# Where the token sums of products by seven are made, and which tiles become such products, in a one-layer Hyena and attention kernel

## The chip, the core and the metric

The kernel runs on one core of one Trainium2 chip. The core has five engines that each take their own instructions in order and wait for one another by semaphores: TensorE (PE, matrix products into PSUM), VectorE (DVE, elementwise work), ScalarE (ACT, copies, tanh, exp), GpSimd (POOL) and SyncE (SP, which issues most DMAs). The metric is the device time of one execution in microseconds. Before the change it is 885.33 us, the median of three runs (885.21 to 885.59).

## The reference, cut to what matters

One layer of a network with two parallel branches, for 128 context tokens and 512 latent tokens (640 columns in all, `NT`), model width 1024:

```python
h = x * (1 + scale) + shift
(v_h, x1, x0, g_h), (q, k, v, g_a), m = split_projection(h, w_in, conv_w, conv_b)
y_h = hyena_long_conv(v_h, x1, x0, h_fwd, h_bwd, hyena_d)
y_a = neighbourhood_attention(q, k, v, ctx_k, ctx_v, rpb)   # the context tokens: context_attention
p_h = (y_h * silu(g_h)) @ w_bh
p_a = (y_a * silu(g_a)) @ w_ba
out = (sigmoid(m)[h] * p_h + sigmoid(m)[a] * p_a) @ w_out
x_new = layer_norm(ALPHA * x + gate * out)
```

`w_in` has 80 tiles of 128 output columns: 32 for the Hyena branch, then 8 each for queries, keys, values, attention gates and the two mixing gates. Everything is float32.

## The kernel before, in words

**Precision.** Each float32 operand of a product is split into a high part (`fp32r`, which the matrix engine multiplies in one pass) and a low part, the rest. A product is three passes: high by high, high by low, low by high. A plain tile of 128 output columns for 640 tokens is 8 blocks of the inner dimension x 3 passes x 2 halves of 320 tokens = 48 matmuls (`accumulate`, L168; with the low passes last, L182). The weight's split costs an ACT copy (high) and a DVE subtraction (low) on 128x1024 (`split`, L100 to L102). With `eng="dma"` (`wtile`, L145 to L149) ACT writes the negated weight into the low tile, ACT writes the high tile, and a DMA issued by POOL adds the weight from memory into the low tile, so that DVE does nothing. Raw tiles have two buffers, high tiles two, low tiles three.

**Products by seven.** `pair_tile` (L1110) makes two weight tiles together by a Strassen-like scheme on 2 x 2 blocks (two halves of the inner dimension, two weight tiles, two halves of the tokens): 7 products of 12 matmuls, 84 in place of 96. It needs sums of token blocks (`token_sums`, L1026, t1 to t4, each with a high and a low part, in two rounds r = 0 and 1 of two blocks each) and sums of weight blocks (`prepare` and `wsum`, L1078 to L1108, all four on DVE). The seven products come in the order b11, t2, t3, t1, b21, t4, b22 (`ORDER`, L1069); b's are the tokens themselves. The weight sums of a pair named in `runs` (L1186) are made in advance, when the pair ahead of it has done its fourth product; a first pair of a run makes its own when it starts. Before the change the 8 mixing pairs, query and key 3 to 7 (one pair each) and the gate pairs from 2 to 7 are made so: 16 pairs.

**Order of the work.** After a prologue (modulation, hidden layers of the filters, first tiles), four quarters of the Hyena branch run: projections, short convolution, and a long convolution by small Fourier matrices (`long_conv`, `long_conv_back`). The last quarter's long convolution is woven (`weave`, L68: so many steps of the side work per step of the main work) into `hand_over` (L841): the last projections, then query 0, key 0, values 0, gate 0, query 1 as plain tiles, then values 1 and key 1 with round 0 of the token sums beside them. `attention_setup` (L854), which comes last in the side chain, gives the convolution's memory back (`hy.close()`) and opens the pools `sp`, `tp` and `at` there; the scratch rows of the token sums (L1034) lie in `sp`, the bias tiles in `at`. Then the attention stage (L1254) goes through eight pairs of heads; the main work of each, `mains(j)` (L1242), is woven with scores, softmax and values. In the first of them, gate 1, query 2 and key 2 are plain tiles with round 1 of the token sums beside them. After attention come the two branch projections, the output projection and the norm.

In the attention stage PE's order is as the program writes it (`manual_schedule`); elsewhere, and on the other engines except for pinned instructions, a scheduler chooses the order when the program is built, by its own model of durations, and the engines then keep to it. So the instruction order of both programs on each engine is known without running them.

Of the kernel before, what the change touches and what calls it, by code (L numbers as in the profile page):

```python
# [18 lines left out]
NK = 8  # L19
# [26 lines left out]
def tile_hyena_natten_step(ctx: ExitStack, tc: tile.TileContext, a, o):  # L46
# [668 lines left out]
    def chain(*gens):  # L715
        for g in gens:
            yield from g
# [47 lines left out]
            nc.vector.scalar_tensor_tensor(ql[:, cs], src[:, ss], scale(cs), f(q[:, cs]), op0=ALU.mult, op1=ALU.subtract)  # L765

    def queries(j):
        for hf, p in enumerate((yield from proj(T_Q + j, low_last=True))):
            q_half(j, hf, p[:, :HALF])
        yield  # L770

# [27 lines left out]

    def keys(j):  # L800
        cached_keys(j)
        for hf, p in enumerate((yield from proj(T_K + j, low_last=True))):
            k_half(j, hf, p[:, :HALF])
        yield

    def values(m):
        w = [wtile(T_V + 2 * m + i, width=256) for i in range(2)]
        ps = [acc(f"v{m}_{i}") for i in range(2)]
        v = slot(m, "v", f"v{m}")
        out[f"v{m}"] = v  # L810

        def passes(k):
            wh, wl = w[k // 4][0][k % 4], w[k // 4][1][k % 4]
            return ((hH, wh, k == 0, False), (hL, wh, False, False), (hH, wl, False, k == NK - 1))

        for half in range(2):
            ks = range(4 * half, 4 * half + 4)
            for k in ks:
                for x, wk, first, last in passes(k):
                    for t in range(4):  # L820
                        nc.tensor.matmul(  # L821
                            ps[t // 2][:, t % 2 * 256 : t % 2 * 256 + 256], x[:, k, P * t : P * t + P], wk,
                            start=first and t % 2 == 0, stop=last, skip_group_check=True,
                        )
                yield
            if half:
                for i in range(2):
                    nc.scalar.activation(v[:, 512 * i : 512 * i + 512], ps[i][:], AF.Copy)
            else:
                pe = acc(f"ve{m}")  # L830
            for k in ks:
                for x, wk, first, last in passes(k):
                    nc.tensor.matmul(pe[:, :256], x[:, k, P * 4 :], wk, start=first, stop=last, skip_group_check=True)  # L833
            yield
        nc.scalar.activation(v[:, 1024:], pe[:, :256], AF.Copy)
        nc.sync.dma_start(o["new_v"][:, m * 256 : m * 256 + 256], v[:, :256])
        yield
# [3 lines left out]
    def hand_over():  # L841
        yield from quarter_tail(3)
        hwa_stack.close()
        out["slots_l"] = left.enter_context(tc.tile_pool(name="slots_l", bufs=1))
        out["slots_q"] = left.enter_context(tc.tile_pool(name="slots_q", bufs=1))
        yield from chain(queries(0), keys(0), values(0), gate_a(0), queries(1))
        out["slots_r"] = left.enter_context(tc.tile_pool(name="slots_r", bufs=1))
        yield from alongside(chain(values(1), keys(1)), token_sums(0), 2)

    tail = ctx.enter_context(ExitStack())  # L850
    ac = ctx.enter_context(ExitStack())
# [2 lines left out]
    def attention_setup():  # L854
        nonlocal at, sp, tp
        hy.close()
        sp = ac.enter_context(tc.tile_pool(name="sp", bufs=1, side="right"))
        tp = left.enter_context(tc.tile_pool(name="tp", bufs=1))
        at = ac.enter_context(tc.tile_pool(name="at", bufs=1, side="right"))
        biases[0] = [bias_tile(h) for h in range(2)]  # L860
        for b, c in ((0, 0), (3, 320)):
            for h in range(2):
                edges[b, h] = at.tile([P, 384], F32, tag=f"edge{b}{h}", name=f"edge{b}{h}")
                nc.gpsimd.memset(edges[b, h][:, c : c + 64], 0.0)
        yield

    at = sp = tp = None

# [145 lines left out]

    N_ATT = 4

    def gate_a(j):
        out[f"sg{j}"] = sg = at.tile([P, NT], F32, tag="sg", bufs=2, name=f"sg{j}") if j else row(yhp, "yh", "sg0")
        yield from gate_tile(T_GA + j, sg[:], low_last=True)
        yield  # L1020


    SUMS = ("t1", "t3", "t2", "t4")
    tok = {t: [[], []] for t in SUMS}

# [52 lines left out]
    def prepare(i0, i1, pin):  # L1078
# [8 lines left out]

        def wsum(j, x, y, op, dst=None):
            src[j] = dst if dst is not None else row(sp, "s", f"s{j}_{i0}", bufs=2)[:, :512]
            ins = nc.vector.tensor_tensor(src[j], x, y, op=op)  # L1090
            if pin and j == 2:
                tc.keep_in_program_order(ins)

# [88 lines left out]
    def mix_(m):  # L1182
# [1 line left out]
        return t, t + 1  # L1184

    runs = (  # L1186
        (mix_(0), qk_(3), mix_(1), qk_(4), ga_(2)), (mix_(2), qk_(5), mix_(3), ga_(4), qk_(6)),
        (mix_(4), qk_(7), mix_(5), ga_(6), mix_(6), mix_(7)),
    )
    follow = {x: y for run in runs for x, y in zip(run, run[1:])}  # L1190
# [6 lines left out]
        for _ in side:  # L1197
            pass

    weave(hand_over(), chain(long_conv(3), long_conv_back(3), attention_setup()), 6 * NK + N_VALUES, N_CONV + N_BACK + 1)  # L1200

    def yh_home(i):
        if i < 4:
# [37 lines left out]

    def mains(j):  # L1242
        return {
            0: ((alongside(chain(gate_a(1), queries(2), keys(2)), token_sums(1), 2, 5),), 3 * NK),
            1: ((mix(0), queries_keys(3)), 2 * N_PAIR),
            2: ((mix(1), queries_keys(4), gates_a(2)), 3 * N_PAIR),
            3: ((values(2), mix(2)), N_VALUES + N_PAIR),
            4: ((queries_keys(5), mix(3), gates_a(4)), 3 * N_PAIR),
            5: ((queries_keys(6), values(3), mix(4)), N_VALUES + 2 * N_PAIR),
            6: ((queries_keys(7), mix(5), gates_a(6)), 3 * N_PAIR),  # L1250
# [313 lines left out]
```

## Time and profile before

| what | value |
|---|---|
| timed runs | 885.21, 885.33, 885.59 us |
| profiled execution, span from first to last instruction | 883.0 us |
| its own time | not listed apart; 2.3 us lie between its span and the median above |
| PE busy | 871.0 us, 6522 matmuls |
| DVE / ACT / POOL busy | 632.7 / 429.5 / 128.8 us |
| mean granted clock of PE | 0.998 |
| end of the Hyena projections on PE | 308.4 us |
| first attention scores on PE | 386.2 us |
| first matmuls of a product by seven | 411.1 us |

The table takes its first rows from the times and the page, the last three from the chain of waits and the clock from the list of cores. PE's busy time counts a matmul from start to end, and matmuls overlap; what one costs is the distance from one start to the next.

### The profile page before, as it was taken

To read this page: it belongs to the slowest core of one execution; us is meant where nothing else is said; L and a number is where in the kernel's file an instruction comes from. 1 tells how busy PE (TensorE), PEld (TensorE's weight loads), DVE (VectorE), ACT (ScalarE), POOL (GpSimd) and SP (SyncE) were. 2 spreads that over 40 slices of the span, in tenths; PEclk is the share of its full clock that TensorE was granted. 3 is DMA by queue.
4 is the path that set the end of the run, shared out by engine and by line. 5 is a ranking of instruction groups with operands and counts; after the bars stand their busy time and mean duration, and the time that the engine had idled before them with its cause. 6 is when DMAs were issued, how large, how long until landed. Compare 5 with 4: busy or idle time off the path is not lost.

```text
span 883.0 us, 16773 instructions
## 1 busy us (share of the span) xinstructions
PE 871.0 (99%) x6522; PEld 843.5 (96%) x6522; DVE 632.7 (72%) x1247; ACT 429.5 (49%) x919; POOL 128.8 (15%) x130
## 2 busy tenths in 40 slices
PE   8999999999999999999999999999999999999996
PEld 7899999999999999999999999999999999999885
DVE  5576693795668478699787567865788567676656
ACT  4486454655545432356665465555666632243200
POOL 1111010010101000024423222222222200000000
PEclk9999999999999999999999999999999999999999
DMA  9976666565656231253525153433252478545511
GB/s 325 401 164 148 134 136 126 132 140 118 168 112 142 70 108 55 72 195 105 164 80 169 55 152 100 142 105 122 80 181 83 132 285 283 181 152 198 214 64 55
DMA packets 54986, 129.07 MB, mean 146 GB/s; under 512 B 8283, under 2 KB 24283, under 8 KB 54908
## 3 DMA queue, kind: packets, MB, share of 16 engines
q1 hardware_dynamic: 45260, 107.62, 37.1%
q0 software_dynamic: 4032, 14.68, 10.2%
q10 hardware_dynamic: 5616, 5.70, 1.9%
q8 instruction: 51, 0.84, 0.4%
q14 instruction: 27, 0.22, 0.1%
HBM read 113.83 MB, written 14.16 MB: 145 GB/s over the span
## 4 chain that ended last, share of the span: by engine, by line
PE 96%; DMA 3%; DVE 1%; SPq 0%; issue 0%; DVEq 0%
PE mm L168 37%; PE sp L1125 23%; PE mm L182 6%; PE out L1391 6%; PE v L821 5%; PE pt L918 3%; PE s L925 2%; PE s L878 2%; DMA ada<-wada 2%; PE ve L833 1%; DMA xt<-xT 1%; PE yb L158 1%; PE yb L156 1%; PE fl L453 1%; PE yb L157 1%; PE ut L601 1%
## 5 line engine op out<-in xcount | busy, mean ns | idle before, releaser
L1125 PE MATMUL sp<-t,wb 128*128 128x320 f32 x768 | 120.6, 310 | 0.0
L1125 PEld LDWEIGHTS sp<-t,wb 128*128 128x128 f32 x768 | 113.8, 188 | 0.5 <-issue 0.5
L168 PE MATMUL mm<-hL,wh 128*128 128x320 f32 x480 | 113.8, 312 | 0.0
L168 PE MATMUL mm<-hH,wh 128*128 128x320 f32 x480 | 113.3, 312 | 0.3 <-ACT hH L365 0.3
L168 PE MATMUL mm<-hH,wl 128*128 128x320 f32 x480 | 111.4, 310 | 0.0
L1125 PE MATMUL sp<-hH,wb 128*128 128x320 f32 x384 | 93.2, 313 | 0.0
L168 PEld LDWEIGHTS mm<-hH,wh 128*128 128x128 f32 x480 | 80.5, 188 | 2.2 <-issue 1.2
L168 PEld LDWEIGHTS mm<-hL,wh 128*128 128x128 f32 x480 | 81.0, 188 | 1.2 <-DVE hL L373 0.4
L168 PEld LDWEIGHTS mm<-hH,wl 128*128 128x128 f32 x480 | 80.6, 188 | 0.3
L1125 PEld LDWEIGHTS sp<-hH,wb 128*128 128x128 f32 x384 | 66.1, 188 | 1.9 <-issue 1.9
L900 POOL TENSOR_SCALAR p<-p,sm 128x384 f32<-128x384 f32 x32 | 46.5, 1462 | 111.8 <-DVE sm L899 98.1
L101 ACT ACTIVATE wh<-raw 128x1024 fp32r<-128x1024 f32 x31 | 32.8, 1059 | 59.2 <-PE mm L168 23.8
L1125 PE MATMUL sp<-hL,wb 128*128 128x320 f32 x192 | 59.3, 309 | 0.0
L148 POOL DMA_DIRECT2D wl<-wall x28 | 24.3, 869 | 226.6 <-ACT wl L147 159.3
L102 DVE TENSOR_TENSOR wb<-s,wb 128x512 fp32r<-128x512 f32 x64 | 44.0, 701 | 15.8 <-ACT wb L101 15.7
L101 ACT ACTIVATE wb<-s 128x512 fp32r<-128x512 f32 x64 | 39.1, 629 | 27.7 <-DVE s L1090 21.5
L101 ACT ACTIVATE wb<-raw 128x512 fp32r<-128x512 f32 x48 | 30.1, 628 | 34.1 <-PE sp L1125 22.0
L102 DVE TENSOR_TENSOR wl<-raw,wh 128x1024 fp32r<-128x1024 f32 x31 | 37.9, 1221 | 12.0 <-ACT wh L101 11.9
L149 ACT ACTIVATE wh<-raw 128x1024 fp32r<-128x1024 f32 x28 | 29.7, 1060 | 33.1 <-PE mm L168 33.0
L1391 PE MATMUL out<-woh,yhs 128*128 128x512 f32 (+1 forms) x176 | 45.5, 372 | 0.0
L900 POOL TENSOR_SCALAR edge<-edge,sm 128x320 f32<-128x320 f32 x32 | 42.5, 1339 | 1.9 <-DVE sm L899 1.9
L168 PE MATMUL mm<-yhs,wh 128*128 128x320 f32 x224 | 41.9, 309 | 0.0
(364 smaller groups left out, 2160.5 us busy)
## 6 DMA issues: line engine op xcount, KB each, us to landing
raw<-wall SPq DMA_DIRECT2D x93, 512.0 KB, 3.6
wl<-wall POOLq DMA_DIRECT2D x28, 512.0 KB, 5.7
ada<-wada SPq DMA_DIRECT2D x16, 512.0 KB, 6.7
tm<-bias SPq DMA_DIRECT2D x16, 512.0 KB, 4.9
gate<-wgate SPq DMA_DIRECT2D x8, 512.0 KB, 4.0
wo<-wall SPq DMA_DIRECT2D x8, 512.0 KB, 4.5
xt<-xT SPq DMA_DIRECT2D x8, 320.0 KB, 7.0
dec<-decay SPq DMA_DIRECT2D x20, 128.0 KB, 5.1
```

Of the source, the lines that this page charges most:

```text
L101: hi = nc.scalar.activation(dst_h, src, AF.Copy)
L102: return hi, (eng or nc.vector).tensor_tensor(dst_l, src, f(dst_h), op=ALU.subtract)
L148: nc.gpsimd.dma_start(wl, a["wall"][i], accum_op=ALU.add)
L149: nc.scalar.activation(wh, raw[:], AF.Copy)
L168: nc.tensor.matmul(ps[hf][:, :HALF], wt[k], x[:, hf * HALF : (hf + 1) * HALF], start=(i == 0 and k == 0), stop=(i == lead[2] and k == NK - ...
L182: nc.tensor.matmul(p[:, :HALF], w[i // 2][k], (hH, hL)[i % 2][:, k, cs], start=n == 0, stop=n == len(steps) - 1, skip_group_check=True,)
L821: nc.tensor.matmul(ps[t // 2][:, t % 2 * 256 : t % 2 * 256 + 256], x[:, k, P * t : P * t + P], wk, start=first and t % 2 == 0, stop=last, ...
L878: nc.tensor.matmul(dst[h], x[rows(h), qs], y[rows(h), ks], start=i == 0, stop=i == 2, skip_group_check=True)
L900: nc.gpsimd.tensor_scalar_mul(pv, pv, sm[:, 2:3])
L918: nc.tensor.transpose(pt[:, i * P : i * P + P], x, ident)
L1125: nc.tensor.matmul(dst, wk, x(xi, k), start=j < 4 and k == 0 and i == 0, stop=k == 3 and i == 2, skip_group_check=True,)
L1391: ins = nc.tensor.matmul(dst, m[k][:, c0 : c0 + P], w[:, c : c + n], start=(first and k == 0), stop=(last and k == 5), skip_group_check=True,)
```

## The change

- Query 0, key 0 and all values get their low halves by accumulating DMA (`eng="dma"`).
- `hand_over` ends with values 0. `attention_setup` is no longer a step of the woven side chain but is called after it. Then comes a new `first_head`: query 0, key 0 and values 1, with both rounds of the token sums beside them, one step of the sums for each step of the tiles.
- Gates 0 and 1, query and key 1, and query and key 2 become products by seven; `gate_a` for single gate tiles goes. The main work of the first heads is rearranged.
- Of the four weight sums of a pair, sums 3 and 6 are made on POOL.

```diff
     def queries(j):
-        for hf, p in enumerate((yield from proj(T_Q + j, low_last=True))):
+        for hf, p in enumerate((yield from proj(T_Q + j, eng="dma", low_last=True))):
...
     def keys(j):
...
-        for hf, p in enumerate((yield from proj(T_K + j, low_last=True))):
+        for hf, p in enumerate((yield from proj(T_K + j, eng="dma", low_last=True))):
...
     def values(m):
-        w = [wtile(T_V + 2 * m + i, width=256) for i in range(2)]
+        w = [wtile(T_V + 2 * m + i, "dma", width=256) for i in range(2)]
...
-        yield from chain(queries(0), keys(0), values(0), gate_a(0), queries(1))
+        yield from values(0)
+
+    def first_head():
         out["slots_r"] = left.enter_context(tc.tile_pool(name="slots_r", bufs=1))
-        yield from alongside(chain(values(1), keys(1)), token_sums(0), 2)
+        yield from alongside(chain(queries(0), keys(0), values(1)), chain(token_sums(0), token_sums(1)), 1)
...
-            ins = nc.vector.tensor_tensor(src[j], x, y, op=op)
+            ins = (nc.gpsimd if j in (3, 6) else nc.vector).tensor_tensor(src[j], x, y, op=op)
...
     runs = (
-        (mix_(0), qk_(3), mix_(1), qk_(4), ga_(2)), (mix_(2), qk_(5), mix_(3), ga_(4), qk_(6)),
+        (ga_(0), qk_(1), qk_(2), mix_(0), mix_(1), qk_(3), ga_(2)), (mix_(2), qk_(4), qk_(5), mix_(3), ga_(4), qk_(6)),
...
-    weave(hand_over(), chain(long_conv(3), long_conv_back(3), attention_setup()), 6 * NK + N_VALUES, N_CONV + N_BACK + 1)
+    weave(hand_over(), chain(long_conv(3), long_conv_back(3)), 4 * NK + N_VALUES, N_CONV + N_BACK)
+    attention_setup()
+    for _ in first_head():
+        pass
...
-            0: ((alongside(chain(gate_a(1), queries(2), keys(2)), token_sums(1), 2, 5),), 3 * NK),
-            1: ((mix(0), queries_keys(3)), 2 * N_PAIR),
-            2: ((mix(1), queries_keys(4), gates_a(2)), 3 * N_PAIR),
-            3: ((values(2), mix(2)), N_VALUES + N_PAIR),
+            0: ((gates_a(0), queries_keys(1)), 2 * N_PAIR),
+            1: ((queries_keys(2), mix(0)), 2 * N_PAIR),
+            2: ((mix(1), queries_keys(3), gates_a(2)), 3 * N_PAIR),
+            3: ((values(2), mix(2), queries_keys(4)), N_VALUES + 2 * N_PAIR),
```

In the changed program `prepare` and its sums are at L1073 to L1103 (`wsum` at L1085), `pair_tile`'s matmuls at L1120, `token_sums` at L1021 to L1056.

More of the change, by code (lines that the diff above doesn't have):

```diff
@@ L864, in attention_setup @@
                 nc.gpsimd.memset(edges[b, h][:, c : c + 64], 0.0)
-        yield
     at = sp = tp = None
@@ L1015, in tile_hyena_natten_step @@
     N_ATT = 4
[L1017 to L1020, printed above, removed]
     SUMS = ("t1", "t3", "t2", "t4")
```

## The prediction

> **What bounds the kernel now.** I read the page first, then the waits of TensorE (PE), then the chain of work that ended last, and only then the other engines, in the one stretch that the change rebuilds.
>
> ```profile
> span 883.0 us, 16773 instructions
> PE 871.0 (99%) x6522; PEld 843.5 (96%) x6522; DVE 632.7 (72%) x1247; ACT 429.5 (49%) x919; POOL 128.8 (15%) x130
> ```
>
> ```profile
> PE adaT L249 <- DMA ada<-wada: 1.8, 3, 0.9
> PE adaT L266 <- POOL spare L308: 1.5, 1, 1.5
> ```
>
> The second fence is the top of PE's waits (line waited for: us in total, times, longest). The largest entries belong to the prologue and are under 2 us; none comes from the middle of the kernel. The chain of waits says the same and gives PE's pace (start us, us, what):
>
> ```profile
> 308.40 1.32 PE mm L182 x9
> ...
> 373.80 0.87 PE y L696 x8
> ...
> 376.83 1.44 PE ve L833 x12
> ...
> 386.19 1.50 PE s L878 x16
> ...
> 439.48 6.17 PE sp L1125 x42
> ...
> 705.18 91.51 PE mm L168 x624
> ```
>
> So the chain runs on PE without holes. A matmul of 320 columns costs 91.51/624 = 0.147 us (6.17/42 agrees), one of 256 columns 1.44/12 = 0.12, a transpose 0.87/8 = 0.11. The "mean ns" of the page, about 310, is latency and is no price. Any matmul less is time won, and any moment in which PE's next operand is not ready is time lost.
>
> **What is removed.** Three pairs of plain tiles (gates 0 and 1, query and key 1, query and key 2) become products by seven: 3 x 96 matmuls go, 3 x 84 come. That is 36 x 0.147 = **-5.3 us** if PE stays fed. With a span of 883.0, 2.3 us under the median of 885.33, this alone would give 880.0.
>
> **What is moved.** A pair's second product reads t2 of both rounds of token sums (`k // 2` picks the round), so now the first pair, gates 0 and 1, needs all sums of both rounds, and its own weight sums behind them. In before, plain tiles (gate 1, query 2, key 2) covered round 1, and half of round 0 lay beside key 1. The sums' scratch lies in pool `sp`, which opens only when the long convolution has given its memory back. The order in which the changed program issues DVE's work settles where they stand (position, line, output<-input; abridged):
>
> ```
> 400 L102 pl_4 (last half of the last long convolution)
> 401-410 L689, L698, L524, L528 (u and yh, ten instructions)
> 411 L1038 ts<-hH,hL (first token sum)
> ...
> 450 L102 t_11 (t2, round 1, low half)
> 453 L102 t_11 (t4, round 1, low half)
> 454 L1085 s_56 (weight sum 1)
> 455 L102 wb_1 (its low half)
> ```
>
> The same listing gives PE: values 1, the first half of product 0, the back transform's last 18 matmuls, 10 transposes, 18 score matmuls, the second half of product 0, then product 1, which waits for ACT's copy of position 454. DVE takes its instructions in this order, so all 26 sums lie on the path.
>
> *When product 0 is half done.* In before PE went from 308.40 to 386.19, 77.8 us, without a hole. The changed order has, up to that half product, 150 fewer plain matmuls (246 down to 96; 22.0 us), 18 matmuls of 256 columns and 10 transposes not yet done (2.2 and 1.1), and 6 new ones (0.9): 77.8 - 22.0 - 2.2 - 1.1 + 0.9 = 53.4, so 361.8.
>
> *When the long convolution ends.* The groups of DVE between 371 and 412 us and the split's price on both engines (busy us, mean ns):
>
> ```profile
> L102 DVE TENSOR_TENSOR t<-ts,t 128x640 fp32r<-128x640 f32 x8 | 6.7, 834 | 0.8 <-ACT t L101 0.8
> L1032 DVE TENSOR_TENSOR ts<-ts,hH 128x640 f32<-128x640 f32 x4 | 3.4, 859 | 0.0
> L1032 DVE TENSOR_TENSOR ts<-ts,hL 128x640 f32<-128x640 f32 x4 | 3.3, 816 | 0.0
> L698 DVE SCALAR_TENSOR_TENSOR u<-u,hyd,y 128x512 f32<-128x512 f32 x2 | 2.2, 1148 | 0.0
> L893 DVE CUSTOM_DVE_ANT_0 p<-s,tm 128x384 f32<-128x384 f32 x4 | 2.0, 544 | 0.0
> L1045 DVE TENSOR_TENSOR ts<-ts,hH 128x640 f32<-128x640 f32 x2 | 1.9, 931 | 0.1
> L893 DVE CUSTOM_DVE_ANT_0 edge<-s,tm 128x320 f32<-128x320 f32 x4 | 1.8, 478 | 0.0
> L1043 DVE TENSOR_TENSOR ts<-hH,hL 128x640 f32<-128x640 f32 x2 | 1.7, 870 | 0.0
> L1046 DVE TENSOR_TENSOR ts<-ts,hL 128x640 f32<-128x640 f32 x2 | 1.6, 820 | 0.0
> L1050 DVE TENSOR_TENSOR ts<-hH,ts 128x640 f32<-128x640 f32 x2 | 1.6, 818 | 0.0
> L1051 DVE TENSOR_TENSOR ts<-ts,hL 128x640 f32<-128x640 f32 x2 | 1.6, 812 | 0.0
> ...
> L528 DVE TENSOR_TENSOR yh<-yh,u 128x64 f32<-128x64 f32 (+1 forms) x4 | 1.4, 415 | 0.0
> L798 DVE TENSOR_TENSOR kl<-ck,k 128x128 fp32r<-128x128 f32 x4 | 1.3, 356 | 0.0
> ...
> L899 DVE RECIPROCAL sm<-sm 128x1 f32<-128x1 f32 x8 | 0.9, 145 | 0.2 <-ACT p L898 0.2
> L1090 DVE TENSOR_TENSOR s<-s,raw 128x512 f32<-128x512 f32 x1 | 0.7, 693 | 0.0
> ...
> L689 DVE SCALAR_TENSOR_TENSOR u<-u,hyd,yp 128x128 f32<-128x128 f32 x2 | 0.6, 344 | 0.0
> L524 DVE TENSOR_TENSOR yh<-yh,u 128x128 f32<-128x128 f32 x2 | 0.5, 280 | 0.0
> L945 DVE TENSOR_REDUCE smp<-s 128x1 f32<-128x128 f32 x2 | 0.5, 281 | 0.0
> ```
>
> ```profile
> L101 ACT ACTIVATE wb<-s 128x512 fp32r<-128x512 f32 x64 | 39.1, 629 | 27.7 <-DVE s L1090 21.5
> ```
>
> The first transform group's last matmul stands 15 matmuls (2.0 us) before 361.8, at 359.8. Only then are its operand buffers free: copies and subtractions of the next two (0.63 + 2 x 0.65) to 361.7, 12 matmuls to 363.2, beside them copy and subtraction of the last operand (0.63 + 0.69) to 363.8, 6 matmuls to 364.5, a copy (0.4, an estimate from the 0.63 for twice the columns) and 2 + 8 transposes to 366.0. DVE's ten instructions (0.6 + 2.2 + 0.5 + 1.4) start at 365.2 and end at **370.0**.
>
> *From there to position 454.* The 26 sums and low halves are 6.7 + 3.4 + 3.3 + 1.9 + 1.7 + 3 x 1.6 = 21.8 us. Among them stand four of the eight score minima (2.0/2 + 1.8/2 = 1.9), two reductions (0.5), reciprocals (0.5), two L798 (0.7) and two weight sums (1.4). Together 26.8, less about 1.8 because consecutive rows overlap slightly in time: **25.0**. One load adds to it: the bias tiles stand behind the yh stores in SP's queue, which go out at 370.0, and by the row below land 4.9 us later, 375.0, where DVE arrives at about 374.2; I take 1.0. Position 454 then ends at 396.0, ACT's copy at **396.7**, and only then does product 1 start. PE's own work between 361.8 and there is 2.2 + 1.1 + 1.5 (scores) + 0.9 = 5.7 of 34.9 us: **29.2 us** of hole.
>
> ```profile
> tm<-bias SPq DMA_DIRECT2D x16, 512.0 KB, 4.9
> wl<-wall POOLq DMA_DIRECT2D x28, 512.0 KB, 5.7
> ```
>
> **After the hole.** A hole this long has a second price. PE's clock and its first work (windows: times, PE, PEld, DVE, ACT, POOL busy, clock; timeline of the prologue):
>
> ```profile
> 880.00:883.00 3.00, 0.00 (x0) 0.00 (x0) 0.00 (x0) 0.00 (x0) 0.00 (x0) 0.50 0.41 139
> ```
>
> ```profile
> 1.54 3.66 PE L266 MATMUL adaT<-hid 128*128 128x256 f32 x16 [1.54 <-POOL spare L308]
> ```
>
> A few us after the last matmul the granted clock is 0.50, and the first 16 matmuls of the kernel take 3.66/16 = 0.23 us instead of 0.12. So about 3.6 us at half pace follow the hole: 1.8 us lost. The Trainium skill (TensorE: Matmul & The Clock Gate, "What's actually happening") puts both the fall and the recovery at about one window of 3.4 us, which would make an estimate of 1.7 us; the trace agrees, though before has no hole in its middle to show it there.
>
> The third product needs a weight sum that POOL now makes, after another one that waits for product 1's low half:
>
> ```profile
> 31.23 1.38 POOL L300 TENSOR_TENSOR wl<-raw,wh 128x512 fp32r<-128x512 f32 x1 [8.42 <-ACT wh L296]
> ```
>
> ```profile
> 394.59 4.73 POOL L900 TENSOR_SCALAR p<-p,sm 128x384 f32<-128x384 f32 x2
> ...
> 421.88 2.46 POOL L900 TENSOR_SCALAR p<-p,sm 128x384 f32<-128x384 f32 x2
> ```
>
> A POOL operation on 512 columns took 1.38 against 0.69 on DVE, and POOL's rows stretch from 1.23 to 2.37 each where DVE is full of sums. Two of them (2.8 to 4.8), a copy and a subtraction end 5 to 7 us after 396.0, while PE at half pace arrives about 6 us after it: 0.4 us (0 to 3). The Trainium skill (SBUF — State Buffer, "Who interferes with whom") says that a DVE operation with two SBUF inputs and a GpSimd operation that reads SBUF block each other for a whole instruction; the 4.73 against 2.46 fits. In later pairs both sums are begun about six products (6 x 12 x 0.147 = 10.6 us) ahead of their use, so I cost them at nothing; without that cover each pair would pay up to 2 us.
>
> The ten new accumulating DMAs land 5.7 us after issue. In the new order values 0 and 1, query 0 and key 0 have their raw tile a whole tile (7 us or more) ahead; if one is late by 2 us, PE loses it before a point where it waits for DVE anyway. The DVE work that goes (16 low halves, 32 weight sums) lies where PE was never waiting for it, so its gain is nothing.
>
> **The sum.** -5.3 + 29.2 + 1.8 + 0.4 = +26.1. Against the profiled span: 883.0 + 26.1 = 909.1, and with the 2.3 us around it **911.4; I predict 911**. Bounds: DVE may reach the first sum at 368 or 372, its stretch may take 24 or 28 (POOL normalises probabilities beside it), the restart 0 to 5, values 2 and 3 with their DMAs in POOL's queue 0 to 2. Together that is 905 to 920.
>
> **Rivals.**
> ```profile
> 342.86 2.83 DVE L641 TENSOR_TENSOR X<-X,F 128x2560 f32<-128x2560 f32 x1
> ```
>
> 1. *The sums do lie beside the tiles* (the side on which it is not slower). If DVE came to its first sum about 26 us before PE has finished product 0 at 367.5 (361.8 + 5.7), that is before some 342 us, the hole would vanish and 880 remain. For it speaks that the change lists the sums beside query 0, key 0 and values 1; against it the issue order and the memory that the last convolution holds: in before the convolution is still at its spectrum's product at 342.86 (the row above). Break-even is a hole of 5.3 us. Chance 0.04, and 0.01 for a draw.
> 2. *The hole is half filled*: DVE runs the convolution's end much earlier than PE's order suggests, and the hole is 10 to 20 us: 891 to 903. Against it: the relay above is set by PE's own order. 0.06.
> 3. *POOL sums late in every pair*: 19 pairs at 1 to 2 us on top of my sum, 930 to 949. For it: 4.73 us for two operations; against it 10.6 us of lead. By the cited rule of blocking, each of two operations would wait for one DVE operation of 0.7 more, 1.4 us, still inside the lead. 0.05.
> 4. My forecast, 903 to 925: 0.84.
>
> The range 903 to 920 holds a little over 8 in 10 of this. A measurement of this kernel can tell about 0.2% (1.8 us) from no change. Faster 0.04, same 0.01, slower 0.95.
>
> **What would show it.** Right: PE's waits, empty in the middle until now, hold one entry of 20 us or more at product 1 of the first pair, with ACT's wb or DVE as its releaser; the first token sum starts near 370 and the last weight sum before it ends near 396; the clock's row there falls to 0.50 and recovers; from the second pair on PE runs at 0.147 again. Wrong: token sums before 350 us, a hole under 15 us, or PE waits on POOL repeated through the attention stage.

## The result, and the profile after

The changed kernel takes **927.81 us** (median of 4 runs, 926.71 to 928.03), the kernel before 885.27 (4 runs, 884.69 to 885.59): a ratio of 1.0482, 95% interval 1.0469 to 1.0495, or 42.5 us more. The profiled execution has a span of 926.3 us against 883.0, 43.3 us more. The forecast was 911 us with a range of 903 to 920: the side was right, the size was not.

The page of the changed kernel, whose rows answer to the page of before:

```profile
span 926.3 us, 16823 instructions
...
PE 875.2 (94%) x6486; PEld 844.8 (91%) x6486; DVE 637.4 (69%) x1241; ACT 448.2 (48%) x945; POOL 186.2 (20%) x178
...
PE   8999999999999999068999999999999999999996
...
PEclk9999999999999999578999999999999999999999
```

PE has 36 matmuls fewer, as counted, and is 94% busy instead of 99%. The 17th and 18th of the 40 slices (each 23.2 us) show the hole, and in the 17th the granted clock is down to half. PE's waits (line, waited for, us in total, times, longest), of which before had nothing beyond the prologue:

```profile
PE sp L1120 <- ACT wb L101: 28.8, 1, 28.8
PE s L879 <- DVE kl L793: 3.7, 2, 1.9
PE pt L919 <- DVE sm L894: 2.1, 1, 2.1
...
PE v L821 <- DMA wl<-wall: 1.8, 1, 1.8
...
PE s L879 <- DVE u L698: 0.8, 1, 0.8
PE pt L919 <- ACT pts L921: 0.7, 1, 0.7
PE yp L686 <- ACT yep L682: 0.5, 1, 0.5
PE yb L157 <- DVE pl L102: 0.3, 1, 0.3
```

These nine waits are 38.8 us (the unrounded entries of the timeline): 28.8 at product 1 of the first pair (its second product; the first is product 0), 1.6 shortly ahead of it (the rows that end in u, yep and pl), and 8.4 behind it. The account of the span is then: -5.3 us for 36 matmuls, +38.8 us of waits, and by subtraction 43.3 + 5.3 - 38.8 = 9.8 us in which PE works, but more slowly than before. Of the waits the prediction has only the first, and in its bounds that of the values.

VectorE's stretch in the timeline of the changed kernel (start, duration, line, output<-input, in brackets idle time before it and what ended that):

```profile
370.11 0.84 DVE L1038 TENSOR_TENSOR ts<-hH,hL 128x640 f32<-128x640 f32 x1
...
374.89 0.49 DVE L894 CUSTOM_DVE_ANT_0 edge<-s,tm 128x320 f32<-128x320 f32 x1 [0.82 <-DMA tm<-bias]
...
382.16 1.09 DVE L1027 TENSOR_TENSOR ts<-ts,hH 128x640 f32<-128x640 f32 x1
383.28 1.19 DVE L1027 TENSOR_TENSOR ts<-ts,hL 128x640 f32<-128x640 f32 x1
385.27 0.83 DVE L102 TENSOR_TENSOR t<-ts,t 128x640 fp32r<-128x640 f32 x1 [0.80 <-ACT t L101]
...
397.36 0.82 DVE L102 TENSOR_TENSOR t<-ts,t 128x640 fp32r<-128x640 f32 x1 [0.80 <-ACT t L101]
398.21 0.69 DVE L1085 TENSOR_TENSOR s<-s,raw 128x512 f32<-128x512 f32 x1
```

And PE behind it:

```profile
399.62 7.90 PE L1120 MATMUL sp<-t,wb 128*128 128x320 f32 x36 [28.81 <-ACT wb L101]
```

The first token sum stands at 370.1 and weight sum 1 ends at 398.9; between them DVE hardly rests. PE starts product 1 at 399.6, and the 36 matmuls of products 1 to 3 (12 each) take 7.90 instead of 36 x 0.147 = 5.3 us. The windows show the clock (span of the window, then busy us of PE, PEld, DVE, ACT, POOL, then granted clock, DMA share, GB/s):

```profile
370.00:380.00 10.00, 0.81 (x6) 0.55 (x4) 9.18 (x24) 6.66 (x19) 3.17 (x7) 0.70 0.89 308
380.00:390.00 10.00, 0.00 (x0) 0.00 (x0) 8.42 (x13) 2.21 (x3) 3.79 (x3) 0.50 0.00 0
...
400.00:410.00 10.00, 10.00 (x57) 9.39 (x57) 7.48 (x12) 3.70 (x8) 3.34 (x2) 0.77 0.37 105
410.00:420.00 10.00, 7.18 (x47) 6.57 (x46) 8.73 (x24) 6.65 (x16) 4.21 (x4) 0.91 0.18 61
420.00:440.00 20.00, 18.12 (x130) 17.17 (x129) 14.10 (x36) 9.67 (x29) 6.91 (x7) 0.87 0.35 110
440.00:560.00 120.00, 120.00 (x960) 117.12 (x960) 79.11 (x209) 71.43 (x174) 52.64 (x43) 1.00 0.43 132
```

The clock isn't back for good at 410 but only at 440, and from 440 to 560 all is as it was in before. Cut finer, the granted clock is 0.50 from 373.9 to 404.6 us, and later again in three stretches of 3.4 us each:

```profile
418.30:421.70 3.40, 2.84 (x12) 2.87 (x13) 1.45 (x9) 2.70 (x9) 3.04 (x3) 0.50 0.77 236
435.40:438.80 3.40, 3.21 (x24) 2.77 (x26) 2.94 (x9) 1.52 (x6) 0.00 (x0) 0.50 0.41 128
568.50:571.90 3.40, 3.40 (x27) 3.07 (x26) 2.76 (x15) 2.18 (x8) 2.10 (x3) 0.50 0.46 169
```

They begin at the first transposes and at the scores of heads 1 and 4, at most 1.7 us behind a wait of PE. Behind the wait for values 3 there is none (1.00 from 622 to 640 us). A stretch of 3.4 us at half pace costs up to 1.7 us (an estimate from these rows). So there are two questions: is the hole really VectorE's token sums, and where do the other 14 us come from?

### The profile page after: what moved, and what is told of

Same layout as the page of the kernel before. It is cut to its first block, busy times and chain, and to the rows that moved or that the text cites. A ratio compares the mean times of both kernels' runs of the same rounds, so it can differ in the third digit from the quotient of the medians.

```text
span 926.3 us, 16823 instructions
## 1 busy us (share of the span) xinstructions
PE 875.2 (94%) x6486; PEld 844.8 (91%) x6486; DVE 637.4 (69%) x1241; ACT 448.2 (48%) x945; POOL 186.2 (20%) x178
## 3 DMA queue, kind: packets, MB, share of 16 engines
q0 software_dynamic: 5472, 19.93, 13.1%
## 4 chain that ended last, share of the span: by engine, by line
PE 89%; DVE 5%; DMA 4%; ACT 1%; issue 0%; SPq 0%; POOL 0%; DVEq 0%; ACTq 0%; POOLq 0%
PE mm L168 35%; PE sp L1120 24%; PE out L1389 6%; PE v L821 5%; PE s L926 3%; PE pt L919 2%; PE s L879 2%; DMA ada<-wada 2%; PE mm L182 2%; PE ve L833 1%; DMA wl<-wall 1%; DVE ts L1027 1%; DMA xt<-xT 1%; DVE t L102 1%; DVE kl L793 1%; PE yb L157 1%
## 5 line engine op out<-in xcount | busy, mean ns | idle before, releaser
L1120 PE MATMUL sp<-t,wb 128*128 128x320 f32 x912 | 145.3, 314 | 28.8 <-ACT wb L101 28.8
L1120 PEld LDWEIGHTS sp<-t,wb 128*128 128x128 f32 x912 | 137.4, 191 | 29.6 <-ACT wb L101 29.1
L1120 PE MATMUL sp<-hH,wb 128*128 128x320 f32 x456 | 111.8, 315 | 0.0
L1120 PEld LDWEIGHTS sp<-hH,wb 128*128 128x128 f32 x456 | 79.4, 190 | 2.6 <-issue 2.6
L1120 PE MATMUL sp<-hL,wb 128*128 128x320 f32 x228 | 71.0, 311 | 0.0
L102 DVE TENSOR_TENSOR wb<-s,wb 128x512 fp32r<-128x512 f32 x76 | 51.8, 694 | 20.9 <-ACT wb L101 20.2
L1085 POOL TENSOR_TENSOR s<-raw,s 128x512 f32<-128x512 f32 x19 | 29.0, 1524 | 160.9 <-DVE wb L102 108.7
L149 ACT ACTIVATE wh<-raw 128x1024 fp32r<-128x1024 f32 x38 | 40.3, 1060 | 42.0 <-PE mm L168 33.5
L102 DVE TENSOR_TENSOR wb<-raw,wb 128x512 fp32r<-128x512 f32 x57 | 45.5, 799 | 16.7 <-ACT wb L101 16.5
L1120 PEld LDWEIGHTS sp<-hL,wb 128*128 128x128 f32 x228 | 43.4, 190 | 0.0
L147 ACT ACTIVATE wl<-raw 128x1024 fp32r<-128x1024 f32 x38 | 40.7, 1070 | 2.8 <-DMA raw<-wall 2.7
```

The source lines that it names most:

```text
L102: return hi, (eng or nc.vector).tensor_tensor(dst_l, src, f(dst_h), op=ALU.subtract)
L147: nc.scalar.activation(wl, raw[:], AF.Copy, scale=-1.0)
L149: nc.scalar.activation(wh, raw[:], AF.Copy)
L1085: ins = (nc.gpsimd if j in (3, 6) else nc.vector).tensor_tensor(src[j], x, y, op=op)
L1120: nc.tensor.matmul(dst, wk, x(xi, k), start=j < 4 and k == 0 and i == 0, stop=k == 3 and i == 2, skip_group_check=True,)
```

## The experiments

Each is compared with runs of the kernel before on the same chip (medians 884.7 to 885.2). "New order" means the changed order of tiles and token sums.

| run | what | median us | ratio to before, 95% interval |
|---|---|---|---|
| e1 | old order, GpSimd sums and DMA halves | 887.98 | 1.0046 (1.0028 to 1.0064) |
| e2 | new order alone | 922.32 | 1.0419 (1.0401 to 1.0437) |
| e3 | change, weight sums on VectorE | 922.07 | 1.0421 (1.0404 to 1.0439) |
| e4 | change, 14 token additions left out | 914.67 | 1.0329 (1.0308 to 1.0351) |
| e5 | change, keys a pair earlier | 921.22 | 1.0419 (1.0401 to 1.0436) |
| e6 | change, first sums in the convolution | 917.76 | 1.0369 (1.0346 to 1.0392) |
| e7 | old order, one pair | 898.66 | 1.0160 (1.0145 to 1.0175) |
| e8 | change, matmuls in the hole | 932.46 | 1.0541 (1.0521 to 1.0560) |
| e9 | e3 and e5 together, values by VectorE | 919.62 | 1.0386 (1.0356 to 1.0416) |
| e10 | e3, second round on GpSimd | 919.48 | 1.0385 (1.0344 to 1.0427) |
| e11 | e9 with plain tiles as cover | 895.07 | 1.0111 (1.0083 to 1.0139) |
| e12 | old order, DMA halves alone | 886.42 | 1.0010 (0.9998 to 1.0023) |

### Which part of the change costs

**e1**, the kernel before with two of the three parts:

```diff
-            ins = nc.vector.tensor_tensor(src[j], x, y, op=op)
+            ins = (nc.gpsimd if j in (3, 6) else nc.vector).tensor_tensor(src[j], x, y, op=op)
...
-    ... proj(T_Q + j, low_last=True) ... proj(T_K + j, low_last=True) ... wtile(T_V + 2 * m + i, width=256)
+    ... proj(T_Q + j, eng="dma", low_last=True) ... proj(T_K + j, eng="dma", low_last=True) ... wtile(T_V + 2 * m + i, "dma", width=256)
```

> The kernel before, with two of the change's three parts: the third and sixth weight sums on GpSimd, and the low halves of plain queries, keys and values by accumulating DMA. The order of the work stays the old one. Theory (the 42 us come from the new order: token sums and weight sums standing alone on VectorE behind the convolution, then short waits behind it): 885 us, between 884 and 889, of which up to 2 us may be a wait of the plain values for their low half. Rival 1 (GpSimd's weight sums, 1.5 us each instead of 0.7, are late in many pairs): 900 us or more. Rival 2 (the accumulating DMAs stand in GpSimd's queue and cost in several places): 890 to 895 us.

The median is 3.1 us more than before, inside the theory's range. Four of its nine runs took 891.0 to 892.4 us, which is rival 2's range. PE's waits in the profiled run (887.98 us) have one entry that before had not:

```profile
PE v L821 <- DMA wl<-wall: 2.9, 2, 1.5
```

So in the old order these two parts cost 2.5 to 5.7 us by the interval, and both rivals fall as explanations of 42 us. Why four runs took some 4 us more is not shown.

**e2**, the other side: the changed kernel with both parts of e1 taken back.

> The changed kernel with all weight sums back on VectorE and the low halves of plain tiles by VectorE as before; only the new order of the work is left. Theory: within 4 us of the changed kernel, 924 to 930 us (2 us less where the plain values no longer wait for a DMA, up to 3 us more where VectorE gets work back inside the hole). Rival 1: under 910 us. Rival 2: under 920 us.

922.32 us, about 2 us below the theory's range and 2 us above the second rival's (under 920): both ranges missed, but the first rival falls, and the order alone is 37 of the 42 us.

**e3**, the changed kernel with only the weight sums taken back (the first line of the diff of e1, reversed).

> The changed kernel with the weight sums on VectorE alone; the order and the accumulating DMAs stay. Theory: 926 to 930 us, the hole ahead of the first pair's second product 27 to 30 us as before. Rival (GpSimd's sums are late in the backlog behind the hole or in every pair): 908 to 922 us.

922.07 us with a hole of 28.8 us. The time is that of e2 (whose hole is 27.0 us and ends at the same time, 399.7 against 399.8), so the DMA halves cost nothing in the new order that these times could tell. But the theory missed: GpSimd's sums do cost 5.7 us, at the very edge of the rival's range, though PE has no wait for GpSimd in either run.

PE's 6486 matmuls stand in the same order in both runs, so the loss can be read place by place. In the profiled executions (spans 926.3 and 919.9) the changed kernel is later by 0.5 us when its clock is back (404.5), by 2.3 behind the first transposes (421.5), by 2.6 behind head 1 (439.8), by 4.7 behind head 4 (571.7) and by 6.4 at values 3 (633.4), and by no more after that. So the first transposes cost 1.8 us, the scores for which keys 1 and 4 are late 0.3 and 2.1, and values 3 cost 1.7 (PE waits 1.8 us for the DMA's low half instead of 0.2).

How GpSimd's sums hold up VectorE is seen at the low half of key 1 in the timelines of both engines in the changed kernel:

```profile
433.14 2.40 DVE L793 TENSOR_TENSOR kl<-c,k 128x64 fp32r<-128x64 f32 x3
```

```profile
432.36 1.61 POOL L1085 TENSOR_TENSOR s<-raw,s 128x512 f32<-128x512 f32 x1 [9.12 <-DVE wb L102]
433.93 1.26 POOL L1085 TENSOR_TENSOR s<-raw 128x512 f32<-128x512 f32 x1
```

and the same subtractions in e3, with two weight sums now on VectorE between and behind them:

```profile
430.72 0.21 DVE L793 TENSOR_TENSOR kl<-c,k 128x64 fp32r<-128x64 f32 x1
430.86 0.69 DVE L1085 TENSOR_TENSOR s<-raw,s 128x512 f32<-128x512 f32 x1
431.46 0.49 DVE L793 TENSOR_TENSOR kl<-c,k 128x128 fp32r<-128x128 f32 x2
```

Three small subtractions with two SBUF inputs, 0.2 to 0.3 us each in e3, take 2.40 us where GpSimd's two sums run (432.36 to 435.19); for key 4 they take 2.40 us again (564.33). VectorE is faster with a weight sum of its own in the middle (1.23 us from 430.72 to 431.95) than with that sum on GpSimd. PE waits 1.9 us for exactly these halves in the changed kernel, and 0.7 in e3, where another 0.6 for the query's low half follows. The Trainium skill (SBUF — State Buffer, "Who interferes with whom") says that a VectorE operation with two SBUF inputs contends with a GpSimd operation that reads SBUF, and calls the port pair that they share an exclusive lock; the 2.40 against 0.70 us agrees in kind. Ahead of the first transposes the same is seen: an operation of the gates (L548), 0.48 us elsewhere, takes 1.31 us (414.61) beside a weight sum of GpSimd (414.29 to 415.57), and the score minima that the softmax begins with stand behind it.

**e12** asks what the DMA halves do by themselves in the old order.

```diff
-    ... proj(T_Q + j, low_last=True) ... proj(T_K + j, low_last=True) ... wtile(T_V + 2 * m + i, width=256)
+    ... proj(T_Q + j, eng="dma", low_last=True) ... proj(T_K + j, eng="dma", low_last=True) ... wtile(T_V + 2 * m + i, "dma", width=256)
```

> The kernel before with the low halves of plain queries, keys and values by accumulating DMA, and nothing else of the change; the weight sums stay on VectorE. With GpSimd's weight sums as well it took 3.1 us more than the kernel before, and its trace had two waits of values for a low half, 1.5 and 1.4 us. Theory (the DMA itself is in time; it is late where GpSimd's weight sums stand ahead of it in GpSimd's queue): no such wait over 0.5 us, 884 to 886 us. Rival (the accumulating DMA takes longer than VectorE's subtraction by itself): the waits stay, 887 to 889 us.

886.42 us, between the ranges of theory and rival; by its interval this cannot be told from no change. One of the two waits of e1 is gone, one stays, so half of the theory fell:

```profile
PE v L821 <- DMA wl<-wall: 1.4, 1, 1.4
```

Its chain of waits tells why (start, duration, what):

```profile
576.00 7.30 PE sp L1125 x49
583.31 8.16 DMA wl<-wall
```

ACT had the negated copy ready at 581.7, GpSimd issued the DMA at 583.3, behind normalisations of probabilities (L953 and L900, 577.6 to 583.4), and it took 8.2 us to land. The queue is 1.6 us of that, the DMA the rest: nothing of it is GpSimd's weight sums, which this run does not have.

### What makes the hole

**e4** leaves out most of the additions.

```diff
-        nc.vector.tensor_tensor(t2, t2, part(hL, 0, 0), op=ALU.subtract)
...
-        nc.vector.tensor_tensor(t1, part(hH, 1, 1), t1, op=ALU.subtract)
-        nc.vector.tensor_tensor(t1, t1, part(hL, 1, 1), op=ALU.add)
...
-        step(t2, 1, 1, -1)
...
-        step(t2, 1, 0, 1)
```

> The changed kernel with 14 of the 18 additions of the token sums left out (seven of nine in each round; the first two stay, and all splits), so that the seven products are fed with wrong sums. Theory: VectorE's stretch ahead of the first weight sums is shorter by 14 x 0.83 = 11.6 us, the wait at the first pair's second product falls from 28.8 to about 17 us, and the kernel takes 912 to 917 us. Rival (something other than VectorE's stretch ends the hole, or the hole moves on to another late operation): a gain of under 6 us, 922 us or more.

PE's wait at product 1 (the line is L1112 there):

```profile
PE sp L1112 <- ACT wb L101: 16.3, 1, 16.3
```

The hole fell by 12.5 us (28.8 to 16.3) and the kernel by 13.1: 0.83 us an addition and a little more. The hole is VectorE's stretch, as forecast. The short waits behind it stayed as long (keys 3.7, first transposes 1.9, values 1.6), so they aren't made by the hole's length.

**e8** fills the hole with matmuls whose result nobody reads.

```diff
+            if i0 == T_GA and j == 1:
+                fill = aux("fill")[:, :HALF]
+                for n in range(190):
+                    nc.tensor.matmul(fill, wb[0][:, 0, :P], hH[:, n % 8, CS[0]], start=n == 0, stop=n == 189, skip_group_check=True)
```

> The changed kernel with 190 matmuls of 128 x 320 (27.9 us at 0.147) into a bank that nothing uses, between the first and the second product of the first pair, so that TensorE works through the hole; one copy on ScalarE is added behind them. Theory (the hole is VectorE's, and the lowered clock is only a part of what follows it): product 1 starts within 2 us of 399.6, its 36 matmuls take 5.3 instead of 7.9 us, the short waits for VectorE behind it stay or grow as TensorE comes to them earlier: 924 to 927 us. Rival (most of the 16 us behind the hole are the granted clock): 912 to 918 us.

It took 932.46 us, 4.65 more than the changed kernel, because the filler itself came late: it had to wait 4.9 us for a PSUM bank, took 30.3 us instead of 27.9 and so held product 1 back to 405.85, 6.2 us later than in the changed kernel:

```profile
375.54 30.47 PE L1120 MATMUL fill<-hH,wb 128*128 128x320 f32 x190 [4.93 <-DVE sm L894]
405.85 5.43 PE L1124 MATMUL sp<-t,wb 128*128 128x320 f32 x36
```

6.2 us late and 2.5 us faster in the 36 matmuls of products 1 to 3 (5.43 against 7.90) make 3.7 of the 4.65. So the clock's restart behind the hole is worth 2.5 us and no more: the waits for the keys (3.7 us), for the first transposes (1.9) and for values (3.0, two waits) are all there, though PE's clock was 1.00 from 380.8 to 421.7 us. The rival, that filling the hole would win back most of the 16 us behind it, falls; the theory's number (924 to 927) missed too, because of the late filler. The clock has more to it than this restart: in e8 too it falls to 0.50 for 3.4 us at the first transposes (421.7) and at head 4 (571.9).

**e10** gives the second round of token sums to GpSimd, with its weight sums back on VectorE.

```diff
-            for t in (hH, hL):
-                nc.vector.tensor_tensor(dst, dst, part(t, i, j), op=ALU.add if sign > 0 else ALU.subtract)
+            for t in (hH, hL):
+                eng.tensor_tensor(dst, dst, part(t, i, j), op=ALU.add if sign > 0 else ALU.subtract)
...
+        eng = nc.gpsimd if r else nc.vector
...
-        ... chain(token_sums(0), token_sums(1)), 1)
+        ... braid(token_sums(0), token_sums(1)), 1)
```

> The changed kernel with the weight sums on VectorE and the whole second round of token sums on GpSimd, side by side with the first round on VectorE (its two scratch rows come from the slots of query 1). Theory (an operation of VectorE with two SBUF inputs and one of GpSimd hold each other up): the first round's additions on VectorE take clearly more than 0.83 us each, about 1.5 to 2.5 us, and the wait at the first pair's second product stays between 22 and 32 us, the time 916 to 926 us. Rival (the engines work side by side): VectorE's operations stay at 0.83 us, VectorE is done 11 us earlier, GpSimd's 13 operations at 1.75 us each (1.40 x 640 / 512) end about 23 us after the convolution, the wait is 16 to 21 us and the time 908 to 915 us.

919.48 us, a gain of 2.6 us against e3 (the intervals of the ratios overlap) with a hole of 23.6. VectorE's first round, and the GpSimd addition that stands beside it:

```profile
369.75 0.82 DVE L1040 TENSOR_TENSOR ts<-hH,hL 128x640 f32<-128x640 f32 x1
...
370.89 2.10 DVE L1042 TENSOR_TENSOR ts<-ts,hH 128x640 f32<-128x640 f32 x1
373.01 2.04 DVE L1043 TENSOR_TENSOR ts<-ts,hL 128x640 f32<-128x640 f32 x1
374.98 2.15 DVE L1047 TENSOR_TENSOR ts<-hH,ts 128x640 f32<-128x640 f32 x1
```

```profile
372.38 1.99 POOL L1029 TENSOR_TENSOR ts<-ts,hH 128x640 f32<-128x640 f32 x1
```

An addition of this shape takes 0.82 us while GpSimd rests and 2.04 to 2.15 while it adds or subtracts. Two engines do little more than one engine's work here, as the theory said; five of GpSimd's 13 operations were done at 318 to 328 us, beside the convolution.

**e6** moves the first round back into the convolution.

```diff
-        yield from values(0)
+        yield from alongside(values(0), token_sums(0), 1)
...
-        ... chain(token_sums(0), token_sums(1)), 1)
+        ... token_sums(1), 1)
...
-        t1, t2 = (two(row(sp, "s", f"ts{r}{i}", bufs=2)[:]) for i in range(2))
+        t1, t2 = (two((row(sp, "s", f"ts{r}{i}", bufs=2) if r else slot(0, ("q", "ql")[i], f"ts{r}{i}"))[:]) for i in range(2))
```

> The changed kernel with the first round of token sums issued beside the first values, while the long convolution still runs; their two scratch rows are taken from the slots of query 0, which the convolution does not touch. Theory: VectorE has idle time there (between 300 and 340 us it was busy 22 of 40 us), so half of the token sums leave its stretch ahead of the first weight sums: 9 adds, 4 subtractions and 4 copies that they wait for, 11 to 14 us. The wait at the first pair's second product falls from 28.8 to 15 to 18 us, and the kernel takes 912 to 917 us. Rival (VectorE's stretch behind the convolution was only postponed work of the convolution, and the sums are late anyway, or they hold up the convolution): 922 us or more.

917.76 us, 0.8 above the theory's range. The hole fell more than expected, and new waits came:

```profile
PE sp L1120 <- ACT wb L101: 11.9, 1, 11.9
PE ve L833 <- ACT v L828: 5.5, 1, 5.5
...
PE v L821 <- DVE kl L793: 3.2, 1, 3.2
```

16.9 us less at product 1, 8.7 us more in the convolution. The 5.5 (at 367.0) are the rival's: on VectorE the convolution's last operations stand behind the sums, of which the first is at 359.0, only 11 us earlier than in the changed kernel. The 3.2 (at 345.3) are not: values 1 waits for key 0's low half, which stands among the convolution's own operations, ahead of any token sum. Both sides were partly right: the sums fit there only in part.

### What makes the short waits behind the hole

**e5** makes keys 1 and 4 a pair earlier.

```diff
-            0: ((gates_a(0), queries_keys(1)), 2 * N_PAIR),
+            0: ((queries_keys(1), gates_a(0)), 2 * N_PAIR),
...
-            3: ((values(2), mix(2), queries_keys(4)), N_VALUES + 2 * N_PAIR),
+            3: ((values(2), queries_keys(4), mix(2)), N_VALUES + 2 * N_PAIR),
```

> The changed kernel with two pairs of tiles exchanged in two places: query and key 1 ahead of gates 0 and 1, and query and key 4 ahead of the mixing gates 2, so that a whole pair of tiles (84 matmuls, 12.3 us) lies between the last key matmul and the scores that read it. Theory: both waits of scores for a low half of keys (1.9 us each) go, with the slow matmuls behind each (about 1 us each): 922 us, between 920 and 924. Rival (VectorE's backlog is what is late, so something else waits in their place): 926 us or more.

921.22 us, 6.6 less than the changed kernel; both waits for keys are gone, the hole and the first transposes (2.1 us) stay. The gain is larger than the 3.7 us of waits, since the two stretches of halved clock behind these waits are gone as well (1.00 from 421.6 to 912 us), and the wait for values 3 fell from 1.8 to 1.1 us. What such a stretch does is seen in the chain of the changed kernel, at the value product of head 4:

```profile
568.40 2.66 PE s L926 x24
```

and in that of e3, at the same place of head 1 and of head 4:

```profile
434.48 2.76 PE s L926 x24
...
565.25 1.46 PE s L926 x24
```

In e3 two waits of 0.6 and 0.7 us stand at either head in the place of one of 1.9. At head 4 the 24 matmuls then take 1.46 us and the clock stays at 1.00; at head 1 they take 2.76, with the clock at 0.50:

```profile
433.80:437.20 3.40, 3.40 (x29) 2.63 (x27) 2.57 (x11) 2.55 (x9) 1.28 (x3) 0.50 0.46 161
```

So the length of the wait alone does not decide whether the clock falls.

**e9** joins e3 and e5 (and takes the values' low halves from the DMA).

> The changed kernel with the weight sums on VectorE, the low halves of plain values by VectorE, and query and key 1 and 4 a pair earlier. Alone, the first gave 5.7 us and the last 6.6 us. Theory (both act on the same waits: GpSimd's sums stretch the subtractions for the low halves of keys, and the earlier keys make it harmless): the gains do not add up, 917 to 920 us. Rival (two separate causes): 912 to 916 us.

919.62 us: by the medians the gains do not add (5.7 + 6.6 would give 915.5, and the fastest run took 918.14), though the lower end of the interval, 1.0356, is about what adding the ratios gives (1.0358). Both waits for keys are gone, as in e5, but PE waits 2.3 us at the first transposes, where e3 had 1.6. So GpSimd's sums and the late keys overlap at the scores of heads 1 and 4, where a subtraction on the path of a wait is stretched by a neighbour; that they are one cause is not shown.

### How much cover the first pair needs

**e7** puts one pair, gates 0 and 1, into the kernel before, behind all plain queries and keys.

```diff
-        yield from chain(queries(0), keys(0), values(0), gate_a(0), queries(1))
+        yield from chain(queries(0), keys(0), values(0), queries(1))
...
-            0: ((alongside(chain(gate_a(1), queries(2), keys(2)), token_sums(1), 2, 5),), 3 * NK),
+            0: ((alongside(chain(queries(2), keys(2)), token_sums(1), 1, 3), gates_a(0)), 2 * NK + N_PAIR),
```

> The kernel before with one of the three pairs: gates 0 and 1 by seven products behind the plain tiles of queries 1 and 2 and keys 1 and 2, which stay plain. Weight sums on VectorE, low halves as before. 12 matmuls fewer are 1.8 us. Theory: plain tiles of queries and keys 2 still lie beside the second round of token sums (2 tiles of 48 matmuls of 0.147 us, 14 us, where before 3 tiles, 21 us, lay), so the wait at the pair's second product is short or none: 883 to 888 us. Rival (any seven-product pair so early stands behind the token sums): a wait of 10 us or more, 893 us or later.

898.66 us: the theory fell, and the time is the rival's, though its one wait of 10 us or more is two shorter ones. One plain tile fewer ahead of the sums (gate 0) and one fewer beside them (gate 1) were already too much:

```profile
PE mm L182 <- ACT v L828: 6.6, 1, 6.6
PE sp L1125 <- ACT wb L101: 4.2, 1, 4.2
```

PE now reaches the end of the convolution a tile earlier, and VectorE has four token sums ahead of the convolution's last operations (371.4 to 374.6), so ACT's copy of values 1, which waits for the last of these operations (L528) and frees the bank, is late for PE (380.53, where before has it at 380.64 with one tile of work more); then the pair waits for its sums too.

**e11** turns it round: from e9, gates 0 and 1 and query and key 1 become plain tiles again and stand in the hole; only query and key 2 are still made by seven among the early tiles.

```diff
-        ... chain(queries(0), keys(0), values(1)), chain(token_sums(0), token_sums(1)), 1)
+        ... chain(queries(0), keys(0), values(1), queries(1), keys(1)), chain(token_sums(0), token_sums(1)), 1)
...
-            0: ((gates_a(0), queries_keys(1)), 2 * N_PAIR),
+            0: ((gate_a(0), gate_a(1)), 2 * NK),
```

> The changed kernel with gates 0 and 1 and query and key 1 as plain tiles again (low halves by DMA), put between the convolution's end and the first pair, which is then query and key 2; weight sums on VectorE, values by VectorE, query and key 4 a pair earlier. One pair is left of the three: 12 matmuls, 1.8 us, fewer than the kernel before. Theory: four tiles of 7.06 us lie where the hole of 28.8 us was, while VectorE gets their 10 or so operations ahead of the first weight sums, so a wait of 3 to 10 us stays: 887 to 895 us. Rival 1 (the cover is complete): 882 to 885 us, a little under the kernel before. Rival 2 (the token sums yield to the tiles' operations on VectorE and the wait moves on unshortened): 900 us or more.

```profile
PE sp L1125 <- ACT wb L101: 4.9, 1, 4.9
```

895.07 us, at the upper end of the theory's range: 28 us of useful work in the hole of 28.8 leave 4.9 us of it; in the timeline the tiles bring VectorE work of their own that stands among the token sums, gates (L548) and the probabilities of the first head among it. Neither e7 nor e11 beats the kernel before: with one pair in place of two plain tiles, which saves 1.8 us, they are 14 and 10 us slower. No experiment points to a version faster than both kernels.

## Why the prediction was right or wrong, point by point

- **-5.3 us for 36 matmuls: right.** 6522 became 6486, and away from the waits PE kept its 0.147 us (no wait from 440 to 560 us).
- **The hole: right in mechanism, its end 2.9 us late.** Half of product 0 was done at 361.9 (forecast 361.8), the first sum at 370.1 (370.0), the wait for the bias tiles was 0.82 us (1.0). The stretch to weight sum 1 was put at 25.0 + 1.0; it took 28.8, from 370.1 to 398.9. Missing were four waits of VectorE for ACT's high halves (0.61, 0.80, 0.20 and 0.80 us in the timeline: where the copy had nothing between itself and the sum it copies, VectorE waits for it) and two additions beside GpSimd's normalisations (1.09 and 1.19 instead of 0.82). PE also came later, by its three waits of 1.6 us in the back transform and the first scores, so the hole itself was 28.8 against the 29.2 forecast. That the length came so close is in part luck: its end was 2.9 us late, and PE's waits and work ahead of it took about 3 us longer as well. e4 showed that it is the sums'.
- **Restart +1.8: a little small.** 7.90 against 5.28 us is 2.6, and e8, with PE kept at work, gave 2.5 back: the clock was 0.50 for the first 5.0 us of PE's work, not for 3.6. The window of about 3.4 us that the Trainium skill (TensorE: Matmul & The Clock Gate, "What's actually happening") gives would make an estimate of 1.7 us; the trace has more.
- **GpSimd's weight sums +0.4, later pairs nothing: this step failed.** They cost 5.7 us in the new order (e3). The prediction asked only whether the sums are in time for their own product, and they are: PE never waits for one. It had the rule of blocking at hand and applied it to GpSimd's side, 1.4 us inside the lead. What is held up is VectorE's work for others: e3, laid beside the changed kernel, puts 1.8 us at the first transposes, 2.4 at the scores that wait for keys 1 and 4, and 1.7 at values 3.
- **Work behind the hole at full pace: this step failed too.** The sum has only the restart behind the hole, and among its signs the prediction says that PE runs at 0.147 again from the second pair on. There were waits of 2.1 and 0.7 us at the first transposes, 1.9 at the scores of heads 1 and 4, 1.8 at values 3: 8.4 us, and at three of these places a stretch of 3.4 us with the clock at 0.50. Keys 1 and 4 are made last before the scores that read them, which the new `mains` shows: half a product, 0.9 us, lies between. The text priced what moved ahead of the hole and didn't ask how long each moved operand has until its reader. e5 and e9 showed the keys; for the first transposes e4 and e8 only show that they wait whatever the hole's length and the restart. In the timeline VectorE's work for the first pair (L548, L102) stands ahead of the score minima there, but that this backlog is the reason was not tested by itself. Why some waits lower the clock and others do not stays open as well.
- **DMA halves 0 to 2 us: right**, 1.8 us at values 3, 0.2 with the weight sums on VectorE (e3), and then nothing that a time could tell (e2 against e3).
- **The sum.** Forecast +26.1 against a span of 883.0, measured +43.3. The missing 17.2: 8.4 of waits behind the hole, 1.6 ahead of it, -0.4 in it, and 9.8 us of slower work where 1.8 for the restart and 0.4 for GpSimd's sums had been allowed. The terms by cause (5.7 for GpSimd's sums, 2.5 for the restart) overlap with these and do not add to them. Of the 9.8 the restart's part, about 2.5, was isolated by e8. Beside e3, the same 12 matmuls at the first transposes took 2.89 us in the halved clock instead of 1.57, and 25 at head 4 took 3.44 instead of 1.84, which is 2.9 more; the stretch at head 1 can be up to 1.7 (the estimate above). For the rest, some 3 us, no place is shown. Added up, the prediction's own bounds reach from about 907 to 922 rather than from 905 to 920; the result lies outside of either.
- **The rivals.** Sums beside the tiles: no, but for the mechanism of the hole the bound was well put, as e6 and e11 moved it both ways. GpSimd's sums late in every pair: its 930 to 949 lay only 2 us above the result, yet its mechanism is wrong; there is no wait of PE on GpSimd's sums, and taking them away gave 5.7, not 19 to 38; that the number came near is luck.

## What to carry to other kernels

When an order is rebuilt, list for every operand that moves both how long its maker needs and how much work lies between it and its reader; a saved matmul of 0.147 us is nothing against a sum that loses its cover. Sums that are to lie beside plain tiles have to be issued beside them on the engine that makes them: here the memory that their scratch rows take stood in the way, and with other rows for half of them (e6) the first sum came 11 us earlier and half of the gain was lost in the convolution. Work given to GpSimd is not free for VectorE, even where nobody waits for GpSimd.

## What the runs showed of the hardware

A VectorE addition of 128x640 with both inputs in SBUF took 0.82 us alone and 2.04 to 2.15 us beside GpSimd additions and subtractions (e10), so that 13 operations moved to GpSimd shortened the hole by 5.2 us only. TensorE's granted clock was 0.50 not only in the hole and the first 5.0 us of work behind it, but again for 3.4 us at a time around three of four waits of about 2 us; the fourth (1.8 us, values 3) had no such stretch. In e3 two waits of 0.7 and 0.6 us were followed by one at head 1 and by none at head 4, and 24 value matmuls took 2.76 and 1.46 us there. So a short wait can cost up to 1.7 us more than itself (half of 3.4, an estimate), and these runs do not show when.
